# A row-sum kernel: loads ahead of the entry barrier, a first block split over four DMAs, and other pieces at the end

## The chip, the cores and the metric

The kernel runs on one core of a Trainium2 chip. The metric is the device time of one execution in microseconds (us). A profile of an execution gives a span about 1.8 us shorter than that time (164.04 and 162.26 us). In what follows DVE is the vector engine, ACT the scalar engine, POOL a third compute engine that has next to nothing to do here, and SP the sync engine, which issues the loads and the store. A load goes from the chip's main memory (HBM) to the 128 partitions of the on-chip memory (SBUF); 16 DMA engines carry it out in packets, here one for each partition's contiguous bytes (896 packets of 64 KB for seven whole blocks of 128 partitions). A DMA has landed when the last increment of its completion semaphore has come. The entry barrier is the point at which all engines wait for each other before the program proper. Ratios and verdicts use runs in the fast state alone; for the two kernels run a single time the state is unknown.

## The reference

```python
x = np.random.randn(32, 512, 1024).astype(np.float32)   # 67.1 MB
def reference(x, multiplier):                            # multiplier = 0.5
    return (np.sum(x, axis=-1) * multiplier).astype(np.float32)
```

That is 16,384 rows of 4 KB, read once, each giving one number.

## The kernel before

Partition p holds rows 128p to 128p+127, so that neighbouring partitions read addresses 512 KB apart. The rows come in eight blocks of 16 per partition (64 KB in a piece), into three buffers. In a block DVE sums half of the rows with one reduce and ACT takes the other half row by row. The last block is loaded in shrinking pieces, so that little work is left when the last byte lands.

```python
    for b in range(n_blocks - 1):                 # n_blocks = 8, B = 16
        c0 = b * B
        t = x_pool.tile([P, B, D], fp32, name="xb")       # bufs=3
        nc.sync.dma_start(out=t, in_=x_rows[:, c0 : c0 + B, :])
        h = B // 2
        nc.vector.reduce_sum(out=sums[:, c0 : c0 + h], in_=t[:, 0:h, :], ...)
        ...                                        # times 0.5 on DVE
        for r in range(h, B):
            act_row(t, r, c0 + r)                  # ACT, one row each
    ...
    cut = 768
    pieces = [(0, 8), (8, 12), (12, 14), (14, 15)]
    for lo, hi in pieces:
        nc.sync.dma_start(out=t[:, lo:hi, :], in_=x_rows[:, c0 + lo : c0 + hi, :])
    for lo, hi in ((0, cut), (cut, D)):            # the last row in two parts
        nc.sync.dma_start(out=t[:, B - 1, lo:hi], in_=x_rows[:, c0 + B - 1, lo:hi])
    on_act = {4, 5, 6, 7, 10, 11, 13}
    ...                                            # the other rows: DVE, dve_span
    dve_span(t, B - 1, 0, cut, part)
    dve_span(t, B - 1, cut, D, res[:, rows - 1 : rows], start=part)
    nc.sync.dma_start(out=out_view, in_=res)
```

Of the kernel before, what the change touches and what calls it, by code (L numbers as in the profile page):

```python
# [1 line left out]

# [4 lines left out]


@with_exitstack
def kernel(  # L10
    ctx: ExitStack,
    tc: tile.TileContext,
    x: bass.AP,
    multiplier: float,
    out: bass.AP,
):







    nc = tc.nc
    P = nc.NUM_PARTITIONS
    fp32 = mybir.dt.float32
    ADD = mybir.AluOpType.add

    x_flat = x.flatten_outer_dims()
    N, D = x_flat.shape  # L30
    rows = N // P
    x_rows = x_flat.rearrange("(p c) d -> p c d", p=P)
    out_view = out.rearrange("b s -> (b s)").rearrange("(p c) -> p c", p=P)
    mul = float(multiplier)

    B = 16
    n_blocks = rows // B
    assert N == P * rows and rows == n_blocks * B

    x_pool = ctx.enter_context(tc.tile_pool(name="x", bufs=3))  # L40
    res_pool = ctx.enter_context(tc.tile_pool(name="res", bufs=1))
    sums = res_pool.tile([P, rows], fp32, name="sums")
    res = res_pool.tile([P, rows], fp32, name="res")
    part = res_pool.tile([P, 1], fp32, name="part")

    def act_row(t, r, col):
        nc.scalar.activation(  # L47
            out=t[:, r, :],
            in_=t[:, r, :],
            func=mybir.ActivationFunctionType.Copy,  # L50
            scale=mul,
            accum_out=res[:, col : col + 1],
        )

    def dve_span(t, r, lo, hi, dst, start=0.0):
        mid = (lo + hi) // 2
        nc.vector.tensor_tensor_reduce(  # L57
            out=t[:, r, lo:mid],
            in0=t[:, r, lo:mid],
            in1=t[:, r, mid:hi],  # L60
            scale=mul,
            scalar=start,
            op0=ADD,
            op1=ADD,
            accum_out=dst,
        )

    for b in range(n_blocks - 1):
        c0 = b * B
        t = x_pool.tile([P, B, D], fp32, name="xb")  # L70
        nc.sync.dma_start(out=t, in_=x_rows[:, c0 : c0 + B, :])  # L71
        h = B // 2
        nc.vector.reduce_sum(  # L73
            out=sums[:, c0 : c0 + h], in_=t[:, 0:h, :], axis=mybir.AxisListType.X
        )
        nc.vector.tensor_single_scalar(  # L76
            out=res[:, c0 : c0 + h],
            in_=sums[:, c0 : c0 + h],
            scalar=mul,
            op=mybir.AluOpType.mult,  # L80
        )
        for r in range(h, B):
            act_row(t, r, c0 + r)

    c0 = (n_blocks - 1) * B
    t = x_pool.tile([P, B, D], fp32, name="xb")
    cut = 768
    pieces = [(0, 8), (8, 12), (12, 14), (14, 15)]
    for lo, hi in pieces:
        nc.sync.dma_start(out=t[:, lo:hi, :], in_=x_rows[:, c0 + lo : c0 + hi, :])  # L90
    for lo, hi in ((0, cut), (cut, D)):
        nc.sync.dma_start(
            out=t[:, B - 1, lo:hi], in_=x_rows[:, c0 + B - 1, lo:hi]
        )
    on_act = {4, 5, 6, 7, 10, 11, 13}
    for r in range(B - 1):
        if r in on_act:
            act_row(t, r, c0 + r)
        else:
            dve_span(t, r, 0, D, res[:, c0 + r : c0 + r + 1])  # L100
    dve_span(t, B - 1, 0, cut, part)
    dve_span(t, B - 1, cut, D, res[:, rows - 1 : rows], start=part)

    nc.sync.dma_start(out=out_view, in_=res)


# [1 line left out]
_INS = ['x', 'multiplier']  # L108
_OUTS = [((32, 512), 'float32')]

_NUMBERS = {'multiplier': 0.5}


# [26 lines left out]
```

## Time and profile before

| | before |
|---|---|
| device time, median of 6 runs | 163.97 us (163.76 to 164.09) |
| span of the profiled execution | 162.26 us |
| DVE, ACT busy | 42% each |
| first load issued | 0.73 us |
| first reduce starts (block 0 has landed) | 22.88 us |
| last result on DVE, then the store is issued | 159.71, 159.78 us |

The page of the profile shows the kind of limit. The first two lines are the span and the busy time of the engines; then the one load queue with its packets and the share of 16 DMA engines' time that they took; then the chain of work that ended last, by engine and by line.

```profile
span 162.3 us, 234 instructions
...
DVE 68.2 (42%) x34; ACT 67.9 (42%) x127; POOL 0.2 (0%) x4
...
q1 hardware_dynamic: 2016, 67.18, 96.5%
...
DMA 85%; DVE 11%; SPq 1%; issue 0%; DVEq 0%
```

The load queue is busy for 96.5% of the span, and the compute engines wait. So only the head (before the first packet), the tail (after the last) and stretches in which packets take longer than usual can give anything. The DVE share of the chain is no limit: it is a reduce that stands before a load is issued into a queue that already holds two blocks (a block's load lands 49.5 us after its issue, the median of seven, and its eight packets of 2.42 us for each engine are 19.4 us of work).

The chain of the kernel before in order of time (start us, us, what) shows the head: nothing before 0.73 us, then the first issue.

```profile
0.67 0.07 issue
0.73 0.38 SPq L71
1.11 0.05 issue
1.16 41.16 DMA xb<-in_x_dram
```

The windows of the kernel before show how the 16 DMA engines come up. The columns are the stretch and its length, busy time of DVE, ACT and POOL, granted clock, DMA share and GB/s. This view counts a packet whole in the stretch in which it *starts*, so that a stretch at the head can show more than the engines can move. A stretch of half a microsecond has one 64 KB packet start for every 131 GB/s: 1049, 393 and 655 are 8, 3 and 5 engines starting.

```profile
1.00:1.50 0.50, 0.00 (x0) 0.50 (x1) 0.00 (x0) 1.00 0.00 0
1.50:2.00 0.50, 0.00 (x0) 0.50 (x1) 0.00 (x0) 1.00 3.05 1049
2.00:2.50 0.50, 0.00 (x0) 0.01 (x1) 0.00 (x0) 1.00 1.15 393
2.50:3.00 0.50, 0.00 (x0) 0.00 (x0) 0.00 (x0) 1.00 1.73 655
```

The packet records behind this view have the first packet at 1.74 us and the last engine's first packet at 2.90 us.

The timeline of DVE in the tail of the kernel before (start us, us, engine, line, operation, what it waited for) shows the last row in two parts: 768 columns at 158.75, when they have landed, and the other 256 right after, at 159.36.

```profile
158.41 0.08 DVE L57 DVE_READ_ACCUMULATOR2_ANT res<- 128x1 f32 x1
158.75 0.56 DVE L57 CUSTOM_DVE_ANT_0 xb<-xb 128x384 f32<-128x384 f32 x1 [0.26 <-DMA xb<-in_x_dram]
159.24 0.08 DVE L57 DVE_READ_ACCUMULATOR2_ANT part<- 128x1 f32 x1
159.36 0.35 DVE L57 CUSTOM_DVE_ANT_0 xb<-xb,part 128x128 f32<-128x128 f32 x1
```

### The profile page before, as it was taken

The numbers are of one execution on the slowest core, as the hardware profiler recorded it, in microseconds if no ns is written. First come the engines' busy times: TensorE is split into PE (matmuls) and PEld (weight loads), VectorE is DVE, ScalarE is ACT, GpSimd is POOL, SyncE is SP. The second block draws the span as 40 slices with busy tenths as digits, with TensorE's granted clock in tenths as the row PEclk, the third lists the DMA queues.
The fourth block names the chain that finished last, engine by engine and source line by source line (L and its number), as shares of the span: only waits on it lengthen the run. The fifth ranks groups of instructions, "written<-read, shape, count | busy, mean of one in ns | idle before, by whom it ended". The sixth has DMA issues, their size and how long they took to land.

```text
span 162.3 us, 234 instructions
## 1 busy us (share of the span) xinstructions
DVE 68.2 (42%) x34; ACT 67.9 (42%) x127; POOL 0.2 (0%) x4
## 2 busy tenths in 40 slices
DVE  0000039800596007940099101990049700697452
ACT  3000039700595007930099101990039600696870
POOL 0000000000000000000000000000000000000000
DMA  7979979979979979979989998998998997998990
GB/s 258 517 307 469 517 323 452 517 323 452 517 323 452 517 323 452 517 323 452 517 372 406 517 404 372 517 404 372 517 404 372 517 436 339 436 444 384 416 383 21
DMA packets 2017, 67.18 MB, mean 414 GB/s; under 512 B 224, under 2 KB 480, under 8 KB 736
## 3 DMA queue, kind: packets, MB, share of 16 engines
q1 hardware_dynamic: 2016, 67.18, 96.5%
q14 instruction: 1, 0.01, 0.0%
HBM read 67.11 MB, written 0.07 MB: 414 GB/s over the span
## 4 chain that ended last, share of the span: by engine, by line
DMA 85%; DVE 11%; SPq 1%; issue 0%; DVEq 0%
DMA xb<-in_x_dram 85%; DVE sums L73 11%; SPq L90 1%; DVE xb L57 0%; SPq L71 0%; DVE part L57 0%; DVEq L135 0%
## 5 line engine op out<-in xcount | busy, mean ns | idle before, releaser
L47 ACT ACTIVATE xb<-xb 128x1024 f32<-128x1024 f32 x63 | 65.6, 1042 | 89.1 <-DMA xb<-in_x_dram 89.1
L73 DVE TENSOR_REDUCE sums<-xb 128x8 f32<-128x8192 f32 x7 | 60.8, 8686 | 86.1 <-DMA xb<-in_x_dram 86.1
L47 ACT ACTIVATION_READ_ACCUMULATOR xb<-xb 128x1 f32 x63 | 11.7, 186 | 0.0
L57 DVE CUSTOM_DVE_ANT_0 xb<-xb 128x512 f32<-128x512 f32 (+1 forms) x9 | 5.8, 674 | 5.2 <-DMA xb<-in_x_dram 5.2
L47 ACT ACT_TABLE_LOAD x1 | 1.3, 1283 | 0.7 <-PEq L121 0.7
L76 DVE TENSOR_SCALAR res<-sums 128x8 f32<-128x8 f32 x7 | 1.2, 172 | 0.2
L57 DVE DVE_READ_ACCUMULATOR2_ANT res<- 128x1 f32 x9 | 0.7, 81 | 0.0
L57 DVE CUSTOM_DVE_ANT_0 xb<-xb,part 128x128 f32<-128x128 f32 x1 | 0.3, 350 | 0.0
L121 POOL MEMSET const-bfloat16-1.0<- 128x1 bf16 x1 | 0.1, 102 | 0.0
L121 POOL MEMSET const-uint8-127<- 128x1 uint8 x1 | 0.1, 102 | 0.0
L121 POOL MEMSET const-float32-1.0<- 128x1 f32 x1 | 0.1, 99 | 0.0
L121 POOL MEMSET const-float32-0.0<- 128x1 f32 x1 | 0.1, 98 | 0.2 <-issue 0.2
L57 DVE DVE_READ_ACCUMULATOR2_ANT part<- 128x1 f32 x1 | 0.1, 83 | 0.0
## 6 DMA issues: line engine op xcount, KB each, us to landing
xb<-in_x_dram SPq DMA_DIRECT2D x1, 4096.0 KB, 39.7
xb<-in_x_dram SPq DMA_DIRECT2D x1, 2048.0 KB, 44.2
xb<-in_x_dram SPq DMA_DIRECT2D x1, 1024.0 KB, 46.2
xb<-in_x_dram SPq DMA_DIRECT2D x1, 512.0 KB, 46.9
xb<-in_x_dram SPq DMA_DIRECT2D x1, 384.0 KB, 47.4
xb<-in_x_dram SPq DMA_DIRECT2D x1, 128.0 KB, 47.2
xb<-in_x_dram SPq DMA_DIRECT2D x7, 49.5
out_dram<-res SPq DMA_DIRECT2D x1, 64.0 KB, 1.5
```

Of the source, the lines that this page charges most:

```text
L47: nc.scalar.activation(out=t[:, r, :], in_=t[:, r, :], func=mybir.ActivationFunctionType.Copy, scale=mul, accum_out=res[:, col : col + 1],)
L57: nc.vector.tensor_tensor_reduce(out=t[:, r, lo:mid], in0=t[:, r, lo:mid], in1=t[:, r, mid:hi], scale=mul, scalar=start, op0=ADD, op1=ADD, ...
L73: nc.vector.reduce_sum(out=sums[:, c0 : c0 + h], in_=t[:, 0:h, :], axis=mybir.AxisListType.X)
L76: nc.vector.tensor_single_scalar(out=res[:, c0 : c0 + h], in_=sums[:, c0 : c0 + h], scalar=mul, op=mybir.AluOpType.mult,)
L90: nc.sync.dma_start(out=t[:, lo:hi, :], in_=x_rows[:, c0 + lo : c0 + hi, :])
L121: nc = _bacc.Bacc("TRN2", target_bir_lowering=False, num_devices=1)
```

## The change

The intent is to start the stream of loads earlier, to bring all 16 DMA engines to work sooner, and to leave less work behind the last byte. The loads that wait for nothing are lifted out of their block and put ahead of the sync engine's part in the entry barrier. The first block is loaded by four DMAs of every fourth partition. The last block comes in pieces of 8, 5 and 2 rows, then 640 and 384 columns.

```diff
-        nc.sync.dma_start(out=t, in_=x_rows[:, c0 : c0 + B, :])
+        step = 4 if b == 0 else 1
+        for q in range(step):
+            nc.sync.dma_start(
+                out=t[q:P:step], in_=x_rows[q:P:step, c0 : c0 + B, :]
+            )
...
-    cut = 768
-    pieces = [(0, 8), (8, 12), (12, 14), (14, 15)]
+    cut = 640
+    pieces = [(0, 8), (8, 13), (13, 15)]
...
-    on_act = {4, 5, 6, 7, 10, 11, 13}
+    on_act = {4, 5, 6, 7, 11, 12, 14}
...
+    def start_loads_at_entry(nc_):
+        entry, *rest = nc_.main_func.blocks
+        ...                      # lead = SP's loads up to the first that waits
+            entry.instructions = head[:at] + lead + head[at:]   # before SP's drain
+            return
+    nc.at_finalize(start_loads_at_entry)
```

More of the change, by code (lines that the diff above doesn't have):

```diff
@@ L104 @@
     nc.sync.dma_start(out=out_view, in_=res)
+    def start_loads_at_entry(nc_):
+        entry, *rest = nc_.main_func.blocks
+        is_sp = lambda i: i.engine == mybir.EngineType.SP
+        is_load = lambda i: type(i).__name__ == "InstDMACopy"
+        for block in rest:
+            body = list(block.instructions)
+            own = [i for i in body if is_sp(i)]
+            if not any(is_load(i) for i in own):
+                continue
+            lead = []
+            for i in own:
+                if not is_load(i) or i.sync_info.on_wait:
+                    break
+                lead.append(i)
+            names = {i.name for i in lead}
+            block.instructions = [i for i in body if i.name not in names]
+            head = list(entry.instructions)
+            at = next(
+                k for k, i in enumerate(head) if is_sp(i) and type(i).__name__ == "InstDrain"
+            )
+            entry.instructions = head[:at] + lead + head[at:]
+            return
+    nc.at_finalize(start_loads_at_entry)
 _INS = ['x', 'multiplier']
```

## The prediction

> **What bounds the kernel.** One stream of loads. In the trace's packet records 16 DMA engines move 67.1 MB in 64 KB packets of 2.418 us (27.1 GB/s an engine), without gaps within an engine; 64 of them are 154.8 us, the floor. The chain of waits gives DMA 85%; DVE and ACT are 42% busy (busy table) and wait on loads for 86 and 89 us (groups). Only head and tail of the 162.3 us span can give.
>
> **Head, before.** SP waits in the entry barrier until 0.73 us (timeline). The first packet starts at 1.74 us, 1.01 after the issue; the other engines follow one by one, the last at 2.90[...]. First packets take 2.5 to 3.1 us, as if all stood still for 0.6 us near 2.4 to 3.0; they end between 4.7 and 5.5. That spread of 0.8 us is still there in the last landings (158.28 to 159.06)[...].
>
> **Tail, before.** The 768 columns land at 158.73; DVE takes them to 159.36, then 256 columns (landed at 159.06, so DVE limits) to 159.71; then the store, landing in 1.5 us, and the closing barrier.
>
> **What the change does.**
> 1. Six loads without waits are issued ahead of the barrier: the first issue moves from 0.73 to about 0. Worth 0.7 us on the stream's path. The barrier opens some 2 us later (six issues of 0.4 us), which delays only engines that wait 20 us for data anyway.
> 2. Four DMAs of 32 rows: [...]the stagger of 1.16 us should shrink to about 0.3 (an estimate, in proportion). The slowest engine gains 0.4 to 0.9 us, if the standstill stays or goes. The further issues are hidden: an engine has 4.8 us of work from the first.[...] This trace shows all engines at equal full rate, but no 32-row DMA.
> 3. Tail: one packet fewer per row saves about 0.09 us of stream (packets of 16, 8, 4, 3, 1 KB take 611, 309, 159, 124, 46 ns). 640 columns land about 0.27 us earlier than 768 did; DVE needs 0.07 less for them and 0.07 more for the 384. The last DVE result comes about 0.25 us earlier.
>
> Sum: 0.7 + 0.65 + 0.25 = 1.6 us of 163.94.
>
> **Prediction: 162.35 us, 8 in 10 between 161.8 and 163.2.** Faster by over 2%: 0.02; within 2%: 0.95; slower by over 2%: 0.03.
>
> **What will show it.** First issue near 0 and first packet near 1.0 us (step 1); all engines' first packets starting within 0.4 us, and last landings within about 0.4 us (step 2); the last DVE result at about 158.1 us (all steps). The 2.418 us packets stay.
>
> **What would make it wrong.** [...]If memory and not dealing limits the start, step 2 gives nothing (about 163.0).

0.7 + 0.65 + 0.25 = 1.6 us, off 163.94 us, and about 162.35 us are predicted. The 0.65 us of step 2 is the middle of its 0.4 to 0.9. It is the author's estimate from the spread of starts of 1.16 us in the trace of before, taken to shrink with the rows of the first DMA, 32 for 128, on the supposition that rows are dealt out one after another.

## More of the kernel before

From the view of the DMA queue's own waits (who waited for what: us in total, times, longest) two lines matter: the entry barrier, and the wait for the store at the end.

```profile
SPq L135 <- DMA out_dram<-res: 1.1, 1, 1.1
SPq L121 <- PEq L121: 0.7, 1, 0.7
```

## The result, and the profile after

| | before | after |
|---|---|---|
| device time, median of 6 runs | 163.97 us (163.76 to 164.09) | 163.31 us (163.13 to 163.42) |
| ratio of the fast runs | | 0.996, 95% interval 0.9947 to 0.9973 |
| span of the profiled execution | 162.26 us | 161.62 us |
| first load issued | 0.73 us | 0.00 us |
| first packet | 1.74 us | 1.35 us |
| block 0 landed (its last landing) | 22.86 us | 22.75 us |
| last result on DVE | 159.71 us | 159.18 us |
| store issued | 159.78 us | 159.26 us |

A ratio is the mean time of one kernel's fast runs over that of the other's in the same rounds, so it is not quite the ratio of the medians quoted. The interval excludes 1. The gain is 0.66 us where 1.6 was predicted, just outside the predicted range of 161.8 to 163.2.

The page after, with the same lines:

```profile
span 161.6 us, 242 instructions
...
DVE 68.1 (42%) x34; ACT 67.9 (42%) x127; POOL 0.2 (0%) x4
...
q1 hardware_dynamic: 1920, 67.18, 96.7%
...
DMA 85%; DVE 11%; SPq 2%; issue 0%; DVEq 0%
```

The head of the chain of the kernel after, in order of time:

```profile
0.00 0.54 SPq L73
0.54 0.06 issue
0.60 0.57 SPq L73
1.17 0.04 issue
1.22 0.59 SPq L73
1.81 0.04 issue
1.85 0.76 SPq L73
2.61 0.04 issue
2.65 39.43 DMA xb<-in_x_dram
```

The first issue is at zero, as intended. But it lasts 0.54 us instead of 0.38, and the four issues of the first block take until 2.61 us.

The windows of the kernel after:

```profile
1.00:1.50 0.50, 0.00 (x0) 0.00 (x0) 0.00 (x0) 1.00 0.72 262
1.50:2.00 0.50, 0.00 (x0) 0.00 (x0) 0.00 (x0) 1.00 2.19 786
2.00:2.50 0.50, 0.00 (x0) 0.00 (x0) 0.00 (x0) 1.00 2.07 786
2.50:3.00 0.50, 0.00 (x0) 0.00 (x0) 0.00 (x0) 1.00 0.61 262
```

The engines start 2, 6, 6 and 2 at a time, still over more than a microsecond, and the last one hardly sooner than before. Of 0.73 us won at the issue, 0.39 is left at the first packet and 0.11 when block 0 has landed.

DVE's timeline in the tail of the kernel after:

```profile
157.98 0.08 DVE L57 DVE_READ_ACCUMULATOR2_ANT res<- 128x1 f32 x1
158.18 0.49 DVE L57 CUSTOM_DVE_ANT_0 xb<-xb 128x320 f32<-128x320 f32 x1
158.59 0.08 DVE L57 DVE_READ_ACCUMULATOR2_ANT part<- 128x1 f32 x1
158.76 0.42 DVE L57 CUSTOM_DVE_ANT_0 xb<-xb,part 128x192 f32<-128x192 f32 x1
```

And the queue's waits in the kernel after. The entry barrier costs SP 0.2 us instead of 0.7, late and off the path. The wait for the store is shorter too, 0.9 us for 1.1, though the store itself lands 1.55 us after its issue in both kernels. This is taken up below.

```profile
SPq L167 <- DMA out_dram<-res: 0.9, 1, 0.9
...
SPq L153 <- PEq L153: 0.2, 1, 0.2
```

### The profile page after: what moved, and what is told of

It is laid out like the page before. It is cut to its first block, busy times and chain, and to the rows that moved or that the text cites. A ratio compares the mean times of both kernels' runs of the same rounds, so it can differ in the third digit from the quotient of the medians.

```text
span 161.6 us, 242 instructions
## 1 busy us (share of the span) xinstructions
DVE 68.1 (42%) x34; ACT 67.9 (42%) x127; POOL 0.2 (0%) x4
## 4 chain that ended last, share of the span: by engine, by line
DMA 85%; DVE 11%; SPq 2%; issue 0%; DVEq 0%
DMA xb<-in_x_dram 85%; DVE sums L77 11%; SPq L73 2%; SPq L94 1%; DVE xb L57 1%; DVE part L57 0%; DVEq L167 0%
```

## The experiments

Each profiled span is cut at marks that every kernel has: the last landing of block 0 (head), the start of the last reduce, when block 6 has landed (middle), the issue of the store (tail), the end (close). "First packet" and "spread" are from the packet records: the start of the first packet, and the time from there until the last of the 16 engines starts its own first packet. The numbers of all runs but e7b stand in a table after the last experiment.

### Which part spoils the head: the early place or the four DMAs (e1 to e4)

Theory E: the early place does it, since engines and sequencer are not ready at that time. Theory R, its rival: the 32-row DMAs do it. Four kernels take the change apart.

e1: only the loads ahead of the barrier. From the kernel before:

```diff
     nc.sync.dma_start(out=out_view, in_=res)
+    nc.at_finalize(start_loads_at_entry)
```

> Only the three loads without waits are moved ahead of the entry barrier; first block in one DMA, old tail. Theory E (the early place is what spoils the head: engines or sequencer are not ready so early): first issue lasts about 0.54 us instead of 0.38, first packet about 1.35 us after the issue instead of 1.01, gain only 0.3 to 0.4 us. Theory R (the 32-row DMAs spoil it): first issue 0.38 us, first packet 1.0 us after issue, stagger 1.16 us as before, gain the full 0.7 us.

Measured: 163.29 us against 163.86 before, ratio 0.9968 (0.9954 to 0.9981), which is a gain of 0.3 to 0.75 us. The first issue lasts 0.38 us, the first packet comes at 1.02 us and block 0 has landed at 22.33 us, 0.53 earlier than before. Theory E has fallen. The windows of this kernel show 9 engines starting in the first half microsecond and 7 in the next:

```profile
1.00:1.50 0.50, 0.00 (x0) 0.00 (x0) 0.00 (x0) 1.00 3.58 1180
1.50:2.00 0.50, 0.00 (x0) 0.28 (x1) 0.00 (x0) 1.00 2.75 918
```

e2: only the four DMAs of the first block.

```diff
-        nc.sync.dma_start(out=t, in_=x_rows[:, c0 : c0 + B, :])
+        step = 4 if b == 0 else 1
+        for q in range(step):
+            nc.sync.dma_start(out=t[q:P:step], in_=x_rows[q:P:step, c0 : c0 + B, :])
```

> Only the first block in four DMAs of every fourth partition, behind the barrier. Theory E: first packet 1.0 us after issue, starts of the 16 engines within about 0.3 us, gain 0.4 to 0.9 us. Theory R: first packet about 1.35 us after issue, starts spread over about 1.3 us, no gain or a loss up to 0.3 us.

Measured: 164.14 us against 163.86, ratio 1.0018 (1.0005 to 1.003): a small loss, and the interval excludes no change. The first packet comes 1.34 us after the issue, the starts are spread over 1.21 us, and block 0 has landed at 23.23 us, 0.37 later than before. This is what theory R said.

e3: only the pieces at the end.

```diff
-    cut = 768
-    pieces = [(0, 8), (8, 12), (12, 14), (14, 15)]
+    cut = 640
+    pieces = [(0, 8), (8, 13), (13, 15)]
-    on_act = {4, 5, 6, 7, 10, 11, 13}
+    on_act = {4, 5, 6, 7, 11, 12, 14}
```

> Only the new pieces at the end. The prediction had 0.25 us for this; if that term was right, 163.7 us. From the after trace, the last result came 0.55 us after the last landing instead of 0.65, so at least 0.1 us; under 0.1 us would mean the tail term was wrong.

Measured: 163.77 us, ratio 0.9996 (0.9983 to 1.0008), so the timed runs do not tell. The marks do: from the start of the last reduce to the issue of the store it is 20.36 us with the old pieces and 20.20 with the new ones, to within 0.04 us in all kernels of the table but one (e14, 20.26). The tail gives 0.16 us.

e4: entry and four DMAs together, old tail (the edits of e1 and e2).

> Entry and four DMAs together, old tail: the whole change less the tail. If the parts add, gain is the 0.66 us of the whole change less that of the tail alone: 0.4 us if the tail gives 0.25. If it exceeds the sum of the two head parts alone, the parts help each other; if below, they get in each other's way.

Measured: 163.46 us, ratio 0.9976 (0.9963 to 0.9989), a gain of 0.4 us. The sum of e1 and e2 is 0.57 - 0.28 = 0.29 us. The parts simply add, within the noise.

### Is it 32 rows, or every fourth partition (e5b)

```diff
-                out=t[q:P:step], in_=x_rows[q:P:step, c0 : c0 + B, :]
+                out=t[q * n : (q + 1) * n], in_=x_rows[q * n : (q + 1) * n, c0 : c0 + B, :]
```

with n = P // step, which is 32 in the first block, on e4.

> Loads ahead of the barrier, first block in four DMAs of 32 neighbouring partitions (0-31, 32-63, ...) instead of every fourth; old tail. If the choice of every fourth partition matters[...], the first block's packets now take about 4.8 us instead of 2.42 and the kernel loses up to 19 us against the one with every fourth (163.46): about 180 us. If an engine's partitions do not matter, the same as every fourth within 0.3 us. It also shows whether the longer issue (0.54 us) comes from the step of four (then 0.38 us here) or from 32 rows (then 0.54 us here).

Measured: 183.89 us, ratio 1.1224. Two things follow. First, if one splits by partitions, it matters which go together: every fourth keeps the full rate (every second too, in e15 below, where block 0 has landed at 22.61 us), 32 neighbours do not. The windows of e4, then of this kernel, from 10 to 30 us:

```profile
10.00:20.00 10.00, 0.00 (x0) 0.00 (x0) 0.00 (x0) 1.00 1.02 439
20.00:30.00 10.00, 7.26 (x1) 7.28 (x12) 0.00 (x0) 1.00 0.97 419
```

```profile
10.00:20.00 10.00, 0.00 (x0) 0.00 (x0) 0.00 (x0) 1.00 1.02 210
20.00:30.00 10.00, 0.00 (x0) 0.00 (x0) 0.00 (x0) 1.00 1.01 210
```

The DMA engines are as busy as before and move half as much: 64 KB packets take 5.12 us instead of 2.42 until block 0 has landed at 43.24 us. A full busy share is thus no proof of full rate. Why 32 neighbours get half the rate no trace shows: the doubling in the expectation was the author's assumption, and measured is a factor of 2.1. Second, the issue of 32 neighbouring rows lasts 0.38 us and the first packet comes at 1.01 us. So neither the 32 rows nor the number of DMAs makes the issue long; the step does.

### Why the engines start one after another (e6b, e7b)

The prediction took the spread of the starts for the dealing of rows: fewer rows in the first DMA, less spread. e2 refuted the size of that (32 rows, 1.21 us). e6b keeps 128 rows and makes the first packets small, on e1:

```diff
-        nc.sync.dma_start(out=t, in_=x_rows[:, c0 : c0 + B, :])
+        cuts = [0, 1, B] if b == 0 else [0, B]
+        for lo, hi in zip(cuts, cuts[1:]):
+            nc.sync.dma_start(out=t[:, lo:hi, :], in_=x_rows[:, c0 + lo : c0 + hi, :])
```

> Loads ahead of the barrier; of the first block one row of 4 KB per partition as a DMA of its own, then the other 15 rows; old tail. If the spread of the first packets' starts (0.8 us in the kernel with only the early place) is the dealing of 128 rows, it is seen again. If it comes from 64 KB reads being started in a cold memory path, the 4 KB packets start within 0.2 us. If the extra 0.65 us of each first packet is a standstill of the path at that time, it shows on whichever packets run then; if it is a start-up cost of the first packet, on the 4 KB packets. Time within 0.3 us of the kernel with only the early place (163.29).

Measured: 162.94 us, ratio 0.994 (0.9925 to 0.9955), already faster than the changed kernel's 163.31, without its tail. With all 128 rows dealt, the 16 engines start within 0.49 us, not within 0.2 and not within 0.8. (Later expectations say 0.38 us for this: a first count took two engines' second packets for first ones.) So dealing 128 rows doesn't need 1.2 us; with 64 KB packets the start is longer. The extra time is shared out: the engines' first 4 KB packets take 0.25 to 0.51 us instead of 0.16, and the 60 KB packets behind them 2.27 to 2.90 instead of 2.27. Block 0 has landed at 22.02 us, 0.3 earlier than in e1.

e7b asks whether this is a cold start of the program. The kernel before gets one buffer, so that every block's load is issued onto idle engines.

```diff
-    x_pool = ctx.enter_context(tc.tile_pool(name="x", bufs=3))
+    x_pool = ctx.enter_context(tc.tile_pool(name="x", bufs=1))
```

> The kernel before with one x buffer instead of three: every load is issued onto idle DMA engines. Much slower, about 240 us (8 times 19.4 us of load, 9 us of reduce and some 1.5 us of start). If the spread of 1.2 us in starts and the 3.05 us first packets are a cold start of the program, later blocks start within 0.3 us and at 2.42 us a packet. If they belong to every load issued onto idle engines, every block shows them.

Measured: 245.5 us (one run, state unknown). The windows around the load that is issued at 62.86 us show the same 8, 3 and 5 starting engines as at the head of the kernel before:

```profile
63.50:64.00 0.50, 0.00 (x0) 0.00 (x0) 0.00 (x0) 1.00 3.16 1049
64.00:64.50 0.50, 0.00 (x0) 0.00 (x0) 0.00 (x0) 1.00 1.24 393
64.50:65.00 0.50, 0.00 (x0) 0.00 (x0) 0.00 (x0) 1.00 1.92 655
```

In all seven 64 KB blocks the first packet comes 0.96 to 1.00 us after the issue, the starts spread over 0.90 to 1.30 us, and the first 16 packets take 2.4 to 3.5 us. The start-up cost belongs to every load issued onto idle engines, and is nothing special to the program's start. The prediction's "standstill near 2.4 to 3.0 us" was this cost, seen once and tied to a time.

### What is left without the four DMAs, and where they do no harm (e8b, e9)

e8b is the change without the four DMAs: the edits of e1 and e3.

> The change without the four DMAs: loads ahead of the barrier and new tail. If the parts add: 163.86 - 0.57 - 0.09 = 163.2 us, against 163.31 of the whole change; it would then beat both by 0.1 to 0.3 us. If the four DMAs cost nothing beside the tail, the same as the whole change.

Measured: 163.12 us, ratio 0.9954 (0.9942 to 0.9967). The parts add; whether it beats the whole change is taken up in e13 and e14.

e9 gives the four DMAs to block 1, on e1.

```diff
-        nc.sync.dma_start(out=t, in_=x_rows[:, c0 : c0 + B, :])
+        step = 4 if b == 1 else 1
+        for q in range(step):
+            nc.sync.dma_start(out=t[q:P:step], in_=x_rows[q:P:step, c0 : c0 + B, :])
```

> Loads ahead of the barrier, the four DMAs of every fourth partition given to the second block instead of the first; old tail. If the loss of the four DMAs is only their longer issue and later first packet, it is hidden here behind the 19 us that the first block takes: the same as the kernel with only the early place, 163.29. If the loss lies in the rows of the block (more semaphore writes, uneven engines), it stays: about 163.46 or more.

Measured: 163.17 us, ratio 0.9954 (0.9941 to 0.9966), no slower than e1 (163.29). Block 0 has landed at 22.33 us as in e1. Behind a queue with 19 us of work the four DMAs cost nothing that shows; their cost is in the start. One thing came unasked: the first packet comes at 1.23 us here instead of 1.02, though the first DMA is the same as in e1; only the DMA issued behind it has the step.

### How large the first packets should be (e10 to e12)

e10 is e6b with `cuts = [0, 4, B]`.

> As the kernel with one 4 KB row first, but four rows (16 KB a partition) in the first DMA and 12 in the second; old tail. If the spread of the starts follows the size of the first packets, it lies between 0.38 us (4 KB) and 0.82 us (64 KB), and the time between 162.94 and 163.29. If only the splitting in two DMAs matters, 0.38 us and 162.94 again.

Measured: 163.09 us, ratio 0.9949 (0.9936 to 0.9961). The expectation missed: the spread is 0.85 us, no less than with 64 KB, yet block 0 has landed at 21.89 us, no later than in e6b. So what a small first piece gains (some 0.3 us at block 0) doesn't go by the spread of the starts alone. The spread is a sign of the start-up cost and not its measure.

e11 is e6b with the new tail, e12 the same with `cuts = [0, 1, 3, 7, B]`.

> Loads ahead of the barrier, one 4 KB row of the first block first, new tail, no DMAs of every fourth partition. If the parts add: 162.94 less about 0.15 for the tail, 162.8 us, faster than the whole change (163.31) by 0.5 us.

> As before but the first block in 1, 2, 4 and 9 rows. If large packets onto engines that are still coming up are what costs, growing them step by step also removes the slow 60 KB packets (2.27 to 2.90 us) that followed the 4 KB row: 162.5 us, up to 0.3 better than with one row first. If the cost of the start has been paid in full by the first small packets, the same as with one row first, 162.8, or 0.1 worse for two more issues.

Measured: 162.93 us, ratio 0.9935 (0.9921 to 0.9948), and 162.97 us, ratio 0.9941 (0.9928 to 0.9954). Both are the fastest correct kernels together with e6b. Growing the pieces step by step adds nothing: block 0 has landed at 21.92 and 21.91 us. The tail's 0.16 us cannot be seen against e6b in time, since in these profiles the middle took 116.98 us where e6b's took 116.15. Nothing in the code of the middle differs. What made it longer stays open; but the profiled execution was the slowest of the five in each of e10, e11 and e12 (163.35, 163.37 and 163.24 us, where the other four average 163.04, 162.87 and 162.90), so the long middle seems to belong to those executions and not to every run of these kernels.

### Within the whole change, and which step costs (e13 to e18)

e13 is the changed kernel again and e14 the kernel of e8b, on one chip.

> The changed kernel once more, beside the next one on the same chip. If the four DMAs cost within the whole change what they cost alone: 0.2 to 0.4 us slower than the next run, block 0 landed at about 22.75 us against 22.2. If the difference of the earlier runs (163.31 against 163.12) was chance of different chips: equal within 0.1 us.

> The change without the four DMAs, on the same chip as the run before: 163.1 us, 0.2 to 0.4 below it; block 0 landed at about 22.2 us.

Measured: 163.24 and 163.14 us, ratios 0.9955 (0.9941 to 0.9968) and 0.9954 (0.9942 to 0.9967). In time the two are the same. In the profiles block 0 has landed at 22.76 and 22.18 us, so the loss of 0.58 us in the head is there; the spans are 161.61 and 161.24 us. Part of it is given back at the close: 2.37 us against 2.55 (below). The remaining 0.3 to 0.4 us is not in the timed runs, and their scatter doesn't explain that. Over all batches, each run taken against the mean of before in its own batch, the 17 runs of the changed kernel (the first result, e13 and e18) gain 0.71 us and the 10 runs of e8b and e14 gain 0.75, a difference of 0.03 us, give or take some 0.15. So beside the new tail the loss in the head is seen on the marks, which come from one profiled execution of each kernel, but not in the time. Why stays open.

e15 has two DMAs of every second partition (`step = 2`) in the whole change.

> The whole change with two DMAs of every second partition (64 rows each) in place of four of every fourth. If any step in the partitions makes the issue longer, the first issue lasts about 0.54 us and the first packet comes at 1.35 us, as with four. If it grows with the step or falls with the rows, it lies between 0.38 and 0.54 us. Time between that of the two runs before.

Measured: 163.4 us, ratio 0.9971 (0.9957 to 0.9985). The issue lasts 0.55 us and the first packet comes at 1.33 us, as with four: a step of two costs as much as a step of four.

e16 keeps the step in the partitions and reads 32 neighbouring input rows. Its output is wrong, which doesn't matter for the time.

```diff
-                out=t[q:P:step], in_=x_rows[q:P:step, c0 : c0 + B, :]
+                out=t[q:P:step], in_=x_rows[q * (P // step) : (q + 1) * (P // step), c0 : c0 + B, :]
```

> A wrong result on purpose: the partitions are still every fourth, but the input rows read are 32 neighbouring ones, so rows land in the wrong partitions. If the partition step in SBUF makes the issue long, still 0.54 us and the first packet at 1.35 us; if the row step in the input does, 0.38 us and 1.0 us.[...]

Measured: 163.0 us (one run, state unknown). The issue still lasts 0.54 us and the first packet comes at 1.32 us: the partition step is enough to make the issue long. But block 0 had landed at 22.24 us, half a microsecond before the change. e17 repeats it beside e18, a third run of the changed kernel.

> Wrong result on purpose, as before: every fourth partition, neighbouring input rows. If the input's row step costs 0.4 to 0.5 us of the first block: block 0 landed near 22.24 us again and the time 0.3 to 0.5 us below the next run's. If the one look was chance: block 0 landed at 22.5 to 22.8 us and times equal within 0.15 us.

> The changed kernel a third time as partner of the run before: 163.25 us, block 0 landed at about 22.75 us, first packet 1.33 us after the issue.

Measured: 162.98 us, ratio 0.9938 (0.9923 to 0.9952), and 163.2 us, ratio 0.9951 (0.9937 to 0.9966). Block 0 had landed at 22.23 us again, against 22.55. The windows of e17, then of e18: with neighbouring input rows 10 and 6 engines start and all are up by 2 us; with every fourth it is 7, 4 and 5.

```profile
1.00:1.50 0.50, 0.00 (x0) 0.00 (x0) 0.00 (x0) 1.00 3.90 1311
1.50:2.00 0.50, 0.00 (x0) 0.00 (x0) 0.00 (x0) 1.00 2.30 786
2.00:2.50 0.50, 0.00 (x0) 0.00 (x0) 0.00 (x0) 1.00 0.00 0
```

```profile
1.00:1.50 0.50, 0.00 (x0) 0.00 (x0) 0.00 (x0) 1.00 2.65 918
1.50:2.00 0.50, 0.00 (x0) 0.00 (x0) 0.00 (x0) 1.00 1.58 524
2.00:2.50 0.50, 0.00 (x0) 0.00 (x0) 0.00 (x0) 1.00 1.79 655
```

The two kernels differ only in which input rows the first block reads together: 512 KB apart or 2 MB apart. So at least part of the start-up loss is made on the reading side. The loss is seen at the start only; once running, packets take 2.42 us with either step (419 GB/s in the window from 10 to 20 us of e17, 426 in e18's). The marks of the profiles show it, two against four. The times agree: e17 and e18 ran on one chip in one batch, and each of the five runs of e17 (162.90 to 163.08 us) is faster than each of the six of e18 (163.13 to 163.32), by 0.22 us on average. That the intervals of their ratios overlap comes from the scatter of before, which stands in both.

### All runs

The profiled execution of each kernel, in us (e7b is left out: each of its loads waits until the block before is summed, so that its middle and tail compare with no other). "Loads" is the number of load DMAs; "first packet" counts from the span's start, which is also the first issue except in before, e2 and e3 (issue at 0.73).

| kernel | loads | first issue lasts | first packet | spread of starts | head: block 0 landed | middle | tail | close |
|---|---|---|---|---|---|---|---|---|
| before | 13 | 0.38 | 1.74 | 1.16 | 22.86 | 116.56 | 20.36 | 2.48 |
| after | 15 | 0.54 | 1.35 | 1.33 | 22.75 | 116.32 | 20.19 | 2.36 |
| e1 entry | 13 | 0.38 | 1.02 | 0.82 | 22.33 | 116.49 | 20.37 | 2.49 |
| e2 four | 16 | 0.55 | 2.07 | 1.21 | 23.23 | 116.25 | 20.36 | 2.41 |
| e3 tail | 12 | 0.36 | 1.73 | 0.79 | 22.97 | 116.20 | 20.20 | 2.56 |
| e4 entry, four | 16 | 0.54 | 1.34 | 1.57 | 22.62 | 116.47 | 20.35 | 2.41 |
| e5b 32 neighbours | 16 | 0.38 | 1.01 | 0.69 | 43.24 | 116.07 | 20.36 | 2.40 |
| e6b row first | 14 | 0.37 | 1.00 | 0.49 | 22.02 | 116.15 | 20.39 | 2.42 |
| e8b entry, tail | 12 | 0.36 | 1.00 | 0.92 | 22.16 | 116.41 | 20.20 | 2.56 |
| e9 four on block 1 | 16 | 0.37 | 1.23 | 1.25 | 22.33 | 116.36 | 20.36 | 2.40 |
| e10 four rows first | 14 | 0.36 | 0.99 | 0.85 | 21.89 | 116.87 | 20.39 | 2.42 |
| e11 row first, tail | 13 | 0.38 | 1.00 | 0.49 | 21.92 | 116.98 | 20.20 | 2.49 |
| e12 graded, tail | 15 | 0.36 | 0.98 | 0.53 | 21.91 | 116.98 | 20.21 | 2.35 |
| e13 after again | 15 | 0.54 | 1.32 | 1.51 | 22.76 | 116.28 | 20.20 | 2.37 |
| e14 entry, tail | 12 | 0.37 | 1.00 | 1.25 | 22.18 | 116.25 | 20.26 | 2.55 |
| e15 two of every 2nd | 13 | 0.55 | 1.33 | 1.16 | 22.61 | 116.13 | 20.18 | 2.49 |
| e16 partition step only | 15 | 0.54 | 1.32 | 0.80 | 22.24 | 116.42 | 20.19 | 2.35 |
| e17 the same again | 15 | 0.55 | 1.35 | 0.46 | 22.23 | 116.35 | 20.20 | 2.36 |
| e18 after, third | 15 | 0.55 | 1.33 | 1.10 | 22.55 | 116.29 | 20.20 | 2.36 |

The close goes by the number of loads and by nothing else that these kernels differ in: 12 loads 2.55 to 2.56 us, 13 loads 2.48 to 2.49, 14 loads 2.42, 15 loads 2.35 to 2.37, 16 loads 2.40 to 2.41. The traces of before and after show the reason. At the end SP waits for eight completion semaphores in a fixed order, and the DMAs use them in turn. Waits that stand ahead of the store's own are done while the store is under way; each that stands behind it costs 0.06 us after the store has landed (in before the store has landed at 161.33 us and SP's waits stand at 161.34, 161.41 and 161.47). With 15 loads the store's semaphore is in the last of five such waits, with 13 loads in the third and with 12 in the second.

## Why the prediction was right or wrong, point by point

The prediction was wrong in its size: 162.35 us with a range to 163.2, measured 163.31. That the kernel is bound by one stream of loads, and that the change stays within 2%, was right.

| term, gain in us | predicted | measured on the marks | how |
|---|---|---|---|
| 1, loads ahead of the barrier | 0.7 | 0.70 | block 0 landed: mean of before and e3, 22.92, less mean of e1, e8b and e14, 22.22 |
| 2, four DMAs | 0.65 | -0.45 | block 0 landed: 22.22 less the mean of after, e4, e13 and e18, 22.67 |
| 3, tail | 0.25 | 0.16 | reduce to store, 20.36 less 20.20 |
| close | not in the sum | 0.12 | 2.48 less 2.36 |

These sum to 0.53 us. In the timed runs step 2 costs less than on the marks: 0.28 us alone (e2), 0.17 beside the early loads (e4 against e1), and 0.03, give or take 0.15, in the whole change. In none of these does it gain. For the two profiled executions that were compared first, the four stretches of the spans give 0.11 (head) + 0.24 (middle) + 0.17 (tail) + 0.12 (close) = 0.64 us, the whole of 162.26 - 161.62. The middle's 0.24 us is not credited to the change: over all kernels of the table it ranges from 116.07 to 116.98 us, and of the edits only e9's touches one of its blocks.

- **Step 1 was right.** The issue moved to zero, and in e1, e8b and e14 the first packet came at 1.00 to 1.02 us. The barrier opened at 4.1 us instead of 0.6, which is 3.4 us later where the prediction had some 2, and it cost nothing: the first data comes more than 18 us after that. ACT began block 0 1.28 us late behind its table load, which now stands behind waits for the four DMAs. This delayed one load's issue (32.58 us instead of 31.65) into a queue with more than a block still to move.
- **Step 2 is the step that failed**, in the words of the prediction: "the stagger of 1.16 us should shrink to about 0.3". The spread was 1.10 to 1.57 us in the four runs of it with early loads. Two things stand in its place. (a) A DMA whose partitions have a step needs 0.54 us to issue instead of 0.38, and its first packet comes 1.32 to 1.36 us after the issue instead of 1.00 (e2, e15, e16). The prediction costed the issues with the duration of another shape in the trace (six of 0.4 us) and took the further ones as hidden; the first issue isn't hidden. The later first packet is 0.34 us of the 0.45. What is not separated is how much of it comes from the first DMA itself: in e9 a DMA with a step, issued behind one without, was enough to move the first packet to 1.23 us. (b) From the first packet to the last landing of block 0 the four DMAs take 21.22 to 21.44 us with early loads (21.16 in e2), one DMA 21.16 to 21.31 in e1, e8b and e14 (21.10 to 21.24 in before, e3 and e9): about 0.1 us lost, hardly more than the scatter, instead of 0.65 won. At least part of this goes by how far apart the rows are that are read together. With neighbouring input rows (e16, e17) this stretch fell to 20.88 to 20.91 us, so that some 0.3 us of the hoped-for gain exists, and the step of four in the input loses it.
- The prediction named the alternative itself ("If memory and not dealing limits the start, step 2 gives nothing"), gave it 163.0 us, and didn't weigh it. The trace of before held a hint that was passed over: the store at the end has 128 rows too, and all its 128 packets had started within 0.32 us. These are small packets (512 bytes), and writes, but it already spoke against rows being dealt at 9 ns each (1.16 us over 128 rows).
- **The choice of every fourth partition was right.** It does give all engines their full rate (2.42 us packets in e4, 5.12 in e5b). The runs show the rates, but not which engine wrote which partition.
- **Step 3 was right in kind, mis-sized in its term.** The 640 columns are started 0.22 us earlier against the last reduce (158.75 - 139.42 = 19.33 before, 158.18 - 139.07 = 19.11 after) where 0.27 was predicted, and the shorter first part saves 0.03 us from start to start (0.61 to 0.58), not 0.07. Then the last part costs 0.07 more, as predicted.
- **The close** was not thought of: 0.12 us of the measured gain comes from the number of loads, and has nothing to do with the intent of the change.

What stays open: why a partition step makes the issue longer; why 32 neighbouring partitions get half the rate; how the reading side holds up the first large packets; why the loss in the head doesn't reach the time of the whole change; and why the middle varies by 0.9 us, which hides gains of this size in the timed runs.

A version that is faster than both kernels was found. One 4 KB row of the first block as its own DMA ahead of the barrier, without the four DMAs, gives 162.93 us with the new tail (e11), 0.65% below before. Its interval (0.9921 to 0.9948) only touches that of the change (0.9947 to 0.9973); they were not run on one chip side by side. Over all batches, each run taken against before in its own batch, the 10 runs of e11 and e12 gain 1.00 us and the 17 of the change 0.71: a difference of 0.28 us, give or take some 0.2.

## What to carry to other kernels

When a stream of loads is the limit, look at its first packets one by one, and test a theory of why they come late with the shape of the DMA you mean to issue: an issue time taken from another shape is no estimate for it (here 0.38 us against 0.54). Change one part at a time and cut the span at marks that all versions share, because parts of half a microsecond cancel and a middle that varies by as much hides them. Then ask whether the timed runs show the same: a loss on a mark of one profiled execution need not reach the end. Begin a stream onto idle engines with a small piece over all partitions, rather than with fewer partitions (here block 0 had landed at 22.02 us in e6b, 22.33 in e1 and 22.62 in e4).
